# Thirty-two unused bytes in the constant pool of a one-core encoder layer

## The chip, the cores and the metric

The kernel runs on one core of one Trainium2 chip. The metric is the device time of the whole program in microseconds, here the median of three runs. A profile of one execution stands beside it: for each engine every instruction with its start, its duration, the source line, the tiles it writes and reads, and what ended the idle time before it. TensorE appears in it twice: PE is the streaming of a matmul's moving operand, PEld is the loading of the stationary operand (the weights) of the next matmul, which runs beside it. The other engines are DVE (VectorE), ACT (ScalarE), POOL (GpSimd) and SP, which issues most of the DMAs.

## The reference

One encoder layer is applied to two sequences of 1024 rows and 1024 columns, in fp32. Attention and a Fourier mixing run side by side, then a SwiGLU feed-forward layer follows. The feed-forward layer, which takes most of the time, is this:

```python
D_MODEL, SEQ = 1024, 1024
D_FF = int(math.ceil(8 * D_MODEL / 3 / 256) * 256)      # 2816

def layer(x, c, ...):
    ...
    mix = jnp.concatenate([y_mla, y_four], axis=-1) @ w_out
    x = x + ga1 * mix
    h2 = rmsnorm(x, g_ffn) * (1.0 + sc2) + sh2
    ffn = (jax.nn.silu(h2 @ w_gate) * (h2 @ w_up)) @ w_down
    return x + ga2 * ffn

y_prompt = rmsnorm(layer(x_prompt, c_prompt, ...), g_final)
y_sample = rmsnorm(layer(x_sample, c_sample, ...), g_final)
```

## The kernel before

**Precision.** Every fp32 operand of a large matmul is split into a high part (rounded to the type fp32r) and the rest: `split` (lines 60 to 63) writes `hi` with a ScalarE cast (L62) and `lo` with a VectorE subtraction (L63). A product is then three matmuls into the same PSUM bank, written by `mm3`:

```python
def mm3(out, lh, ll, rh, rl, first, last, cont=False):
    nc.tensor.matmul(out, lh, rh, start=first, stop=False, ...)      # L78
    nc.tensor.matmul(out, lh, rl, start=False, stop=False, ...)      # L79
    nc.tensor.matmul(out, ll, rh, start=False, stop=last, ...)       # L80
```

The second argument of `matmul` is the stationary operand, 128 columns of it; the third is the moving operand, as a rule 512 columns. So lines 78 to 80 carry most of TensorE's work, and the tile names in the profile tell the stages apart.

**Stages.** In order of time: the adaLN vectors, projections and the Fourier sums (0 to about 335 us), attention with the output projection (to about 797 us), then the feed-forward layer for sequence 0 and for sequence 1. Each feed-forward layer has two halves, and both use a Strassen-Winograd scheme, with seven products of half-size matrices in place of eight.

*Gate and up* (797 to 1237 us and 1449 to 1888 us). The seven combinations of the layer's input stand in SBUF for the whole half, each as two tiles of 4 x 512 columns, `H[k][0]` and `H[k][1]` (named H00 to H61, H in the profile). For each of 22 blocks of weights, `combos` loads the tile `rgu` (a slot named X0 or X1) and makes the sums on POOL into tiles `val`; `hl` splits each of the seven into `wh` and `wl`; and `prod` runs twelve matmuls for each of the seven:

```python
def prod(ps, k, wt, first):
    wh, wl = wt
    for c in range(4):
        cs = slice(c * P, c * P + P)
        mm3(ps, wh[:, cs], wl[:, cs], H[k][0][:, c, :], H[k][1][:, c, :], ...)
```

The weights are stationary, H moves. Between the products DVE adds bank and `val` (L137) and ACT copies a bank (L1311) before the same bank is added to again. The splits for block n+1 are written into the program beside the products of block n, so they run one block ahead; there are eight buffers each of `wh` and `wl`.

*Down* (1237 to 1449 us and 1888 us to the end). `prod2` loads two tiles of 512 columns for each step into a slot X0 or X1 (`draw` in the profile), splits both through `hl`, and multiplies `wh`/`wl` of the one by `wh`/`wl` of the other. At the end of sequence 1 the last of the seven products takes its operands, stationary and moving, from tiles that were split in advance into H slots (`held`).

**Where tiles lie.** Tiles come from pools on two sides of SBUF. A pool on the left grows from low addresses: first the constants (`const`), then small scalars (`tiny`), then one stage pool after another, in the feed-forward layer `p5` with the H and X slots. A pool with `side="right"` hangs from the top of SBUF: in the feed-forward layer `p5b` with `val`, `wh`, `wl`, `gf` and `ga`; in attention `p3` with `qa`, `qp`, `p` and `pt`, and `p4` with `wv` and the tiles `o`. The allocator rounds every tile to a multiple of 32 bytes. Addresses of the built program, modulo 64 bytes (and in brackets modulo 512):

| tiles | side | before |
|---|---|---|
| H and X slots (`rgu`, `draw`, `held`) | left | 0 (448) |
| `wh`, `wl`, `val`, `gf`, `ga` | right | 32 (480) |
| `lat00`, `lat01` (keys of sequence 0), `ckv`, `ql`, `wq_h`, `wq_l` | left | 0 (448) |
| `lat10`, `lat11` (keys of sequence 1), `qa`, `qp`, `pt`, `wv`, `o` | right | 32 (480) |
| `wz_h`, `wz_l` (input projection) | left | 0 |
| `hh`, `hl` of even pairs / of odd pairs | left | 0 / 32 |
| `ident` | constant, first tile | 0 |

The 512-column steps of a tile are 2048 bytes and the 128-column steps 512 bytes, so a slice of H, `wh` or `wl` keeps its tile's value.

**Order.** No planner sets the order: the instructions of an engine stand as the program emits them, and the tile framework adds the waits.

Of the kernel before, what the change touches and what calls it, by code (L numbers as in the profile page):

```python
# [12 lines left out]
F32 = mybir.dt.float32  # L13
# [8 lines left out]
P = 128  # L22
# [30 lines left out]
def hybrid_encoder_kernel(ctx: ExitStack, tc: tile.TileContext, a: dict):  # L53
# [28 lines left out]
    const = ctx.enter_context(tc.tile_pool(name="const", bufs=1))  # L82
# [7 lines left out]
    mhalf = const.tile([P, 2], F32, name="mhalf")  # L90
    nc.gpsimd.memset(mhalf, -0.5)
    cmask = const.tile([P, 7], F32, name="cmask")
    nc.sync.dma_start(cmask, a["cmask"])

    def rstd(ms, n, rest=None):
# [1535 lines left out]
```

## Time and profile before

| | |
|---|---|
| time, median of 3 runs | 2117.27 us (2114.76 to 2119.18) |
| span of the profiled execution, first to last instruction | 2109.8 us |
| its own time with what lies around the span | not listed for it; the median less the span is 7.5 us |
| gate and up, sequence 0 / sequence 1 | 797 to 1237 us / 1449 to 1888 us |
| down, sequence 0 / sequence 1 | 1237 to 1449 us / 1888 to 2110 us |
| DMA traffic | 371.30 MB, 176 GB/s over the span |

Rows by line read: line, engine, operation, output<-inputs, shape, xcount | busy us of the group, mean ns of one | idle time of the engine just before them, and what ended it. In rows of matmuls the moving and the stationary tile stand behind the arrow in that order, except that a name that is both stands once; the end of a matmul is modelled, so the mean is longer than the distance from one start to the next, by the same amount for the same shape. Rows by window read: stretch, its length, then for each engine busy us (xcount), the granted TensorE clock, the DMA engines' busy share and GB/s. A window counts each instruction that overlaps it.

### The profile page before, as it was taken

The page shows a single profiled execution, that of the slowest core. Times are in us where ns is not written, and L with a number is a line of the kernel's source. Part 1 is how long each engine was busy: PE and PEld are TensorE (multiplying, and loading weights), DVE is VectorE, ACT ScalarE, POOL GpSimd, SP SyncE. Part 2 cuts the span into 40 slices and gives each one's busy share as a digit, 9 for nine tenths or more (in the row PEclk, how much of TensorE's full clock was granted, in tenths as well). Part 3 has the DMA queues.
Part 4 walks back from the last instruction along what each step waited for, and adds up shares of the span by engine and source line. Part 5 has one row for each costly group of instructions (what it writes and reads, how often), then busy time and mean ns, then how long its engine had stood idle before and what let it go on. Part 6 is the DMA issues. An engine that isn't in the chain of part 4 may idle for free. (4 is left out here: it accounts for less than half of the span.)

```text
span 2109.8 us, 28784 instructions
## 1 busy us (share of the span) xinstructions
PE 2033.0 (96%) x10044; PEld 1667.0 (79%) x10044; DVE 1414.4 (67%) x2087; ACT 906.0 (43%) x1763; POOL 828.6 (39%) x1018
## 2 busy tenths in 40 slices
PE   5899998999999999999999999999999999999998
PEld 2788876888888887788888888887788888888886
DVE  2657756766676678777677677777766666566685
ACT  2656534555565555232333346453233333336441
POOL 1455202111311314888778610235544454420142
PEclk8999999999999999999999999999999999999999
DMA  9575765544544455554554578674332232247772
GB/s 368 194 248 190 248 233 197 113 88 91 159 119 118 150 186 211 180 193 169 194 185 166 174 250 270 222 236 164 131 119 90 91 125 95 81 154 280 233 227 99
DMA packets 184254, 371.30 MB, mean 176 GB/s; under 512 B 19052, under 2 KB 58604, under 8 KB 181036
## 3 DMA queue, kind: packets, MB, share of 16 engines
q1 hardware_dynamic: 166252, 314.00, 44.1%
q0 software_dynamic: 17856, 55.45, 8.9%
q8 instruction: 79, 1.29, 0.2%
q14 instruction: 67, 0.55, 0.1%
HBM read 257.38 MB, written 120.39 MB: 179 GB/s over the span
## 5 line engine op out<-in xcount | busy, mean ns | idle before, releaser
L78 PE MATMUL bank<-H,wh 128*128 128x512 f32 x1232 | 489.6, 398 | 7.7 <-ACT val L1311 4.0
L80 PE MATMUL bank<-H,wl 128*128 128x512 f32 x1232 | 488.9, 397 | 1.4 <-DVE wl L63 1.4
L79 PE MATMUL bank<-H,wh 128*128 128x512 f32 x1232 | 489.0, 397 | 0.0
L137 DVE TENSOR_TENSOR val<-bank,val 128x512 f32<-128x512 f32 x244 | 167.1, 690 | 185.7 <-PE bank L80 178.6
L78 PEld LDWEIGHTS bank<-H,wh 128*128 128x128 f32 x1232 | 232.5, 189 | 66.8 <-ACT val L1311 5.4
L80 PEld LDWEIGHTS bank<-H,wl 128*128 128x128 f32 x1232 | 232.5, 189 | 57.9 <-DVE wl L63 1.7
L79 PEld LDWEIGHTS bank<-H,wh 128*128 128x128 f32 x1232 | 232.7, 189 | 56.2
L63 DVE TENSOR_TENSOR wl<-draw,wh 128x512 fp32r<-128x512 f32 x286 | 203.1, 744 | 82.7 <-ACT wh L62 80.7
L62 ACT CAST wh<-draw 128x512 fp32r<-128x512 f32 x286 | 168.8, 619 | 159.0 <-PE bank L79 83.0
L137 POOL TENSOR_TENSOR val<-val 128x512 f32<-128x512 f32 x58 | 82.9, 1438 | 366.3 <-DVE val L1412 187.6
L79 PE MATMUL bank<-wl,wh 128*128 128x512 f32 x572 | 223.8, 391 | 1.6 <-DVE wl L63 1.6
L80 PE MATMUL bank<-wh,wl 128*128 128x512 f32 x572 | 222.7, 389 | 0.0
L78 PE MATMUL bank<-wh 128*128 128x512 f32 x572 | 222.6, 389 | 0.0
L62 ACT CAST wh<-rgu 128x512 fp32r<-128x512 f32 x172 | 106.7, 621 | 269.7 <-PE bank L79 209.5
L62 ACT CAST wh<-val 128x512 fp32r<-128x512 f32 x133 | 82.2, 622 | 280.5 <-PE bank L79 249.1
L63 DVE TENSOR_TENSOR wl<-val,wh 128x512 fp32r<-128x512 f32 x133 | 141.5, 1066 | 85.6 <-ACT wh L62 85.5
L63 DVE TENSOR_TENSOR wl<-rgu,wh 128x512 fp32r<-128x512 f32 x172 | 169.4, 985 | 4.9 <-ACT wh L62 4.8
L134 POOL TENSOR_TENSOR val<-rgu 128x512 f32<-128x512 f32 x84 | 122.8, 1462 | 125.0 <-DMA rgu<-in_wgu_dram 108.8
L79 PEld LDWEIGHTS bank<-wl,wh 128*128 128x128 f32 x572 | 107.4, 188 | 27.3 <-DVE wl L63 5.3
L78 PEld LDWEIGHTS bank<-wh 128*128 128x128 f32 x572 | 107.4, 188 | 22.4
L80 PEld LDWEIGHTS bank<-wh,wl 128*128 128x128 f32 x572 | 107.4, 188 | 22.0
L134 POOL TENSOR_TENSOR val<-val 128x512 f32<-128x512 f32 x89 | 119.4, 1357 | 1.3
(332 smaller groups left out, 4051.2 us busy)
## 6 DMA issues: line engine op xcount, KB each, us to landing
rgu<-in_wgu_dram SPq DMA_DIRECT2D x86, 512.0 KB
draw<-s_d SPq DMA_DIRECT2D x143, 256.0 KB
s_d<-val POOLq DMA_DIRECT2D x88, 256.0 KB, 4.1
draw<-t_d SPq DMA_DIRECT2D x88, 256.0 KB
s_d<-val SPq DMA_DIRECT2D x66, 256.0 KB
draw<-in_w_down_dram SPq DMA_DIRECT2D x55, 256.0 KB
wada<-in_w_ada_dram SPq DMA_DIRECT2D x13, 1024.0 KB
xt<-in_x_dram SPq DMA_DIRECT2D x16, 512.0 KB
```

The costliest lines, as they stand in the source:

```text
L62: here["a"] = nc.scalar.copy(hi, src).ins
L63: here["v"] = nc.vector.tensor_tensor(out=lo, in0=src, in1=rd(hi), op=ALU.subtract).ins
L78: nc.tensor.matmul(out, lh, rh, start=first, stop=False, skip_group_check=cont)
L79: nc.tensor.matmul(out, lh, rl, start=False, stop=False, skip_group_check=cont)
L80: nc.tensor.matmul(out, ll, rh, start=False, stop=last, skip_group_check=cont)
L134: return eng.tensor_tensor(out=out, in0=x, in1=y, op=ALU.subtract).ins
L137: eng.tensor_tensor(out=out, in0=x, in1=y, op=ALU.add)
```

## The change

One tile of 128 x 8 fp32 (32 bytes in each partition) is added to the pool `const`, behind its first tiles. Nothing writes or reads it.

```diff
     cmask = const.tile([P, 7], F32, name="cmask")
+    const.tile([P, 8], F32, name="phase")
     nc.sync.dma_start(cmask, a["cmask"])
```

Every tile that is allocated behind it on the left side lies 32 bytes higher: 1087 tile allocations, among them every H and X slot, `lat00`, `lat01`, `ckv`, `ql`, `wq_h`, `wq_l`, `wz_h`, `hh` and the small scalars. The tiles on the right side, `ident`, `identr`, `mhalf` and `cmask` stay where they were. Modulo 64, H and X are then at 32 (modulo 512 at 480), as `wh`, `wl` and `val` are, and two left-side tiles keep their distance from each other. All 18430 instructions of the built program, their order on each engine and their operands' tiles and shapes are the same as before; line numbers behind line 92 grow by one.

## The prediction

> **What bounds the kernel now.** I read the page first, for the share of each engine, then the stretches of the feed-forward layer by window, then TensorE's rows by form inside them, and last what TensorE waits for.
>
> ```profile
> span 2109.8 us, 28784 instructions
> PE 2033.0 (96%) x10044; PEld 1667.0 (79%) x10044; DVE 1414.4 (67%) x2087; ACT 906.0 (43%) x1763; POOL 828.6 (39%) x1018
> L78 PE MATMUL bank<-H,wh 128*128 128x512 f32 x1232 | 489.6, 398 | 7.7 <-ACT val L1311 4.0
> ```
>
> TensorE is busy 96% of the span, and gate and up alone are 3 x 1232 = 3696 matmuls of 512 columns (L78 shown; L79 and L80 have as many). The windows tell whether anything else holds them up:
>
> ```profile
> core 0: us, PE busy (x), PEclk, DMA share, GB/s
> 860.00:1230.00 370.00, 370.00 (x1587) 1.00 0.52 179
> 1510.00:1880.00 370.00, 370.00 (x1588) 1.00 0.29 100
> 1240.00:1390.00 150.00, 150.00 (x664) 1.00 0.79 262
> ```
>
> The first two are gate and up of the two sequences, the third is down. TensorE has no idle time in any of them and the clock is fully granted. So a matmul's own spacing sets the time there. It is not the same: a window catches one matmul more than fits, so it is (370.0 + 0.4)/1587 = 233.4 ns in gate and up and (150.0 + 0.4)/664 = 226.5 ns in down. The rows of these windows say it again:
>
> ```profile
> L78 PE MATMUL bank<-H,wh 128*128 128x512 f32 x529 | 209.2, 396 | 0.0
> L80 PE MATMUL bank<-H,wl 128*128 128x512 f32 x529 | 209.2, 395 | 0.0
> L79 PE MATMUL bank<-H,wh 128*128 128x512 f32 x529 | 209.2, 395 | 0.0
> ...
> L79 PE MATMUL bank<-wl,wh 128*128 128x512 f32 x222 | 86.4, 389 | 0.0
> L80 PE MATMUL bank<-wh,wl 128*128 128x512 f32 x221 | 86.0, 389 | 0.0
> L78 PE MATMUL bank<-wh 128*128 128x512 f32 x221 | 86.0, 389 | 0.0
> ```
>
> Same shape, type, clock and order of three; 6 to 7 ns apart. What differs is where the operands lie. In gate and up the moving H is at 0 modulo 64 and the stationary `wh` and `wl` at 32; in down both are at 32. Is it the address, or something else of the stage? Three places tell. The product from `held` runs at the end, with both operands in the very H slots:
>
> ```profile
> L79 PE MATMUL bank<-H 128*128 128x512 f32 x44 | 17.1, 389 | 0.0
> ```
>
> At 0 and 0 it takes 389 again, so H slots are not slow in themselves. The scores of attention are one piece of code that runs on both sequences; only the moving keys change, from `lat00`/`lat01` at 0 (sequence 0, first three rows, 400 to 545 us) to `lat10`/`lat11` at 32 (sequence 1, last three, 550 to 764 us), against `qa` and `qp` at 32:
>
> ```profile
> L906 PE MATMUL ps_s<-lat,qp 128*128 128x512 f32 x39 | 15.4, 395 | 0.0
> L907 PE MATMUL ps_s<-lat,qp 128*128 128x512 f32 x39 | 15.4, 395 | 0.0
> L904 PE MATMUL ps_s<-lat,qa 128*128 128x512 f32 x38 | 15.0, 396 | 0.0
> ...
> L907 PE MATMUL ps_s<-lat,qp 128*128 128x512 f32 x64 | 25.1, 392 | 0.0
> L904 PE MATMUL ps_s<-lat,qa 128*128 128x512 f32 x64 | 25.1, 392 | 0.0
> L906 PE MATMUL ps_s<-lat,qp 128*128 128x512 f32 x64 | 25.0, 391 | 0.0
> ```
>
> Apart 395 to 396, equal 391 to 392: the same sign. And the input projection alternates, at 448 columns: `wz` moves from 0, and the stationary `hh` is at 0 for even pairs (first three rows, 199.9 to 204.5 us) and at 32 for odd ones (218.3 to 222.9 us).
>
> ```profile
> L78 PE MATMUL bank<-wz_h,hh 128*128 128x448 f32 x8 | 2.9, 368 | 0.0
> L79 PE MATMUL bank<-wz_l,hh 128*128 128x448 f32 x8 | 2.9, 368 | 0.0
> L80 PE MATMUL bank<-wz_h,hl 128*128 128x448 f32 x7 | 2.6, 368 | 0.0
> ...
> L78 PE MATMUL bank<-wz_h,hh 128*128 128x448 f32 x8 | 2.9, 363 | 0.0
> L79 PE MATMUL bank<-wz_l,hh 128*128 128x448 f32 x8 | 2.9, 363 | 0.0
> ```
>
> Here equal addresses are the slower case, by 5 ns. So the address matters, but which relation is good depends on the length of the stream. For 512 columns every place that I found says equal is faster.
>
> **The change part by part.** No instruction is added, removed or moved; only addresses change.
>
> *Gate and up.* H goes to 32 modulo 64 and 480 modulo 512, which is what both operands of down have. I take down's spacing. The step per matmul is 6 (395 to 389) to 6.9 ns (233.4 to 226.5); I take 6.6. 3696 x 6.6 ns = 24.4 us if each one gains it. Where TensorE waited, an earlier arrival only lengthens the wait:
>
> ```profile
> PE bank L78 <- ACT val L1311: 4.0, 2, 2.6
> PE bank L78 <- DVE val L137: 3.4, 3, 2.1
> ...
> PE bank L80 <- DVE wl L63: 1.4, 1, 1.4
> ```
>
> Each row is its total, the number of times and the longest: six waits in the whole execution, all outside the windows above, so in the first blocks of a sequence. A block is 84 matmuls, so it gains 84 x 6.6 ns = 0.55 us. At worst six blocks lose their gain, 3.3 us; at best none. A wait takes only what stands ahead of it in its block, so I take half, 1.6 us. Gain 22.8 us.
>
> Can the others keep up with a block of 19.05 instead of 19.6 us?
>
> ```profile
> 850.00:1237.00 387.00, 386.14 (x1655) 310.90 (x1656) 274.39 (x277) 118.26 (x199) 288.40 (x264) 1.00 0.52 177
> ...
> 1500.00:1888.00 388.00, 385.88 (x1648) 310.27 (x1647) 239.78 (x280) 116.92 (x196) 170.50 (x145) 1.00 0.29 103
> ```
>
> In the fuller one, sequence 0 (columns PE, PEld, DVE, ACT, POOL), POOL is busy 288.4 of 387 us, 75%, and DVE 71%. At 2.8% shorter blocks they come to 77% and 73%. The splits run a block ahead, so their cover is about 19 us deep, and rows without idle time show that nothing is late now. I take no new wait; one new wait like those above in every fourth block, at 1 us, would cost 11 us, and that is a rival below.
>
> *Attention.* The scores of sequence 0, five lines of 64 matmuls, get the addresses of sequence 1: 320 x 3.5 ns is 1.1 us. Of that I take 0.8, as TensorE waits now and then in this stage. The value product moves `pt` at 32 against `ckv`, which goes from 0 to 32. It is 768 matmuls of 256 columns, of which no row shows the equal case for these tiles. The nearest with both on the left side, equal before and after, is the absorbed query:
>
> ```profile
> L80 PE MATMUL gb<-pt,ckv 128*128 128x256 f32 x123 | 35.0, 285 | 0.0
> ...
> L80 PE MATMUL gb<-ql,wq_l 128*128 128x256 f32 x30 | 8.5, 284 | 0.0
> ```
>
> 284 equal against 285 apart (both 550 to 760 us): no difference, and I take 0. The bounds are those of the longer streams: 5 ns slower as at 448 columns (3.8 us) to 6.6 ns faster (5.1 us).
>
> *Everything else.* `wz` and `hh`, `ql` and `wq` shift together. The splits of down get both inputs at 32 instead of 0 and 32, and DVE, ACT and POOL read tiles on either side already:
>
> ```profile
> L63 DVE TENSOR_TENSOR wl<-draw,wh 128x512 fp32r<-128x512 f32 x286 | 203.1, 744 | 82.7 <-ACT wh L62 80.7 <-DMA draw<-t_d 1.3
> L63 DVE TENSOR_TENSOR wl<-rgu,wh 128x512 fp32r<-128x512 f32 x172 | 169.4, 985 | 4.9 <-ACT wh L62 4.8
> ...
> L137 DVE TENSOR_TENSOR val<-val 128x512 f32<-128x512 f32 x12 | 8.0, 684 | 0.0
> L63 DVE TENSOR_TENSOR wl<-H,wh 128x512 fp32r<-128x512 f32 x3 | 2.1, 689 | 0.0
> ```
>
> The first two rows are the splits whose addresses change, at means that hold many stretched ones. The last two show a plain subtraction or addition of that shape: equal (32 and 32) 684 ns, apart (0 and 32) 689 ns. DVE doesn't tell them apart by more than 1%, and if the equal case were slower by as much, 286 + 172 splits at 5 ns are 2.3 us of an engine that is busy 71%, under TensorE. DMA writes to the slots start 32 bytes later; their share in down is 0.79, so they could take a quarter longer before they bind. Cost nothing.
>
> *The sum.* 22.8 + 0.8 = 23.6 us less: the profiled span goes from 2109.8 to 2086 us. The median lies 7.5 us over that span, so 2117.3 - 23.6 = 2093.7, and I say 2094.
>
> **The rule that speaks against it.** The Trainium skill's page "TensorE: Matmul & The Clock Gate" (Step-by-step: what each phase is for) says that TensorE reads SBUF through two independent ports, one for the streamed operand and one for the weights, so that loading the next weights takes nothing from the running matmul. By that rule an address cannot matter, and the time would stay at 2117. The rows above, 396 against 389 with one shape and clock, contradict it as far as one execution can.
>
> **The rivals.**
>
> *Nothing happens.* The 6.6 ns belong to the stage and not to the address: while gate and up run, POOL and DVE read the same memory more than in down. For it: I compare stages of different surroundings. Against it: POOL is far busier in sequence 0 than in sequence 1 of gate and up (288 against 170 us in the rows above), yet both windows have 233.4 ns; and the scores differ between sequences by the address alone. Time 2117; 4%.
>
> *Equal is the slow case for H too.* The input projection shows equal addresses 5 ns slower. If a long run over one set of H rows followed that pattern instead of down's, 3696 x 5 ns = 18.5 us are added in gate and up and 3.8 us in the value product: 2140. The mechanism is one, a read of weights that falls on the same part of memory as the streamed row; it decides as soon as the rows `bank<-H,wh` go above 396. Against it stands `held`, which is equal, from H, with 512 columns, at 389. 3%.
>
> *Another engine takes over.* The matmuls get faster, but blocks become uneven: POOL's sums, stores and DVE's splits block each other, and every fourth of 44 blocks waits 1 us. 23.6 - 11 = 12.6 us less: 2105. For it: POOL at 77%, and six such waits are there now. Against it: none after the first blocks of a sequence. 5%.
>
> *The tiles don't move as told.* The built program has them moved, so this is only open where a tile that matters stayed; H did not. It joins the first rival.
>
> **How the numbers follow.** Forecast 88%, rivals 4, 3 and 5%. Its own range: all matmuls gain 6.9 ns, no wait eats any (25.5), scores 1.1, and values gain half of their best (2.5): 29 us, 2088. At the other end 6 ns with six blocks lost (22.2 - 3.3 = 18.9), values lose 3.8: 15 us, 2102. The three runs before spread by 2 us either way, within these. Faster by over 0.2% (4.2 us; about what a measurement of this kernel can tell from no change): forecast and third rival, 93%. Within 0.2%: the first rival, 4%. Slower: 3%.
>
> **What would show it.** Right: rows `bank<-H,wh` and `bank<-H,wl` at 389 instead of 395 to 396; windows inside gate and up without idle time and about 45 matmuls more in 370 us; rows of down, `held` and `wz` as they are; scores of sequence 0 at 391 to 392; no new releaser behind L78. Wrong: H rows still at 395 with all else equal (the address is not the cause), or at 389 with new idle time behind ACT, DVE or POOL (the third rival), or `gb<-pt,ckv` longer by more than 5 ns.

## The result, and the profile after

| | before | after |
|---|---|---|
| time, median of 4 runs | 2116.28 us (2114.76 to 2119.18) | 2098.30 us (2095.19 to 2101.20) |
| ratio after / before, 95% interval | | 0.9918 (0.9906 to 0.9930) |
| span of the profiled execution | 2109.8 us | 2096.1 us (its own time 2097.92) |
| a block of gate and up between the waits | 19.60 us | 19.04 us |

The kernel is 18.0 us faster. The forecast was 2094 us, 23.6 us less, and its range was 2088 to 2102.

The rows of gate and up first, from the groups of the whole page, with the rows of the value product from the list of TensorE's groups (columns as before: busy us, mean ns of one, idle time before):

```profile
L78 PE MATMUL bank<-H,wh 128*128 128x512 f32 x1232 | 483.7, 393 | 10.2 <-ACT val L1312 5.4
L80 PE MATMUL bank<-H,wl 128*128 128x512 f32 x1232 | 482.7, 392 | 1.9 <-DVE wl L63 1.9
L79 PE MATMUL bank<-H,wh 128*128 128x512 f32 x1232 | 482.9, 392 | 0.0
L80 PE MATMUL bank<-wh,wl 128*128 128x512 f32 x572 | 222.8, 389 | 0.0
...
L78 PE MATMUL gb<-pt,ckv 128*128 128x256 f32 x256 | 74.0, 289 | 0.0
L80 PE MATMUL gb<-pt,ckv 128*128 128x256 f32 x256 | 73.5, 287 | 0.0
L79 PE MATMUL gb<-pt,ckv 128*128 128x256 f32 x256 | 73.4, 287 | 0.0
```

The rows of the value product before, over the same 768 matmuls:

```profile
L78 PE MATMUL gb<-pt,ckv 128*128 128x256 f32 x256 | 73.2, 286 | 0.0
L80 PE MATMUL gb<-pt,ckv 128*128 128x256 f32 x256 | 72.8, 284 | 0.0
L79 PE MATMUL gb<-pt,ckv 128*128 128x256 f32 x256 | 72.7, 284 | 0.0
```

The scores of sequence 0 after (400 to 545 us), for the three lines that the prediction showed:

```profile
L907 PE MATMUL ps_s<-lat,qp 128*128 128x512 f32 x40 | 15.6, 391 | 0.0
L908 PE MATMUL ps_s<-lat,qp 128*128 128x512 f32 x40 | 15.6, 391 | 0.0
L905 PE MATMUL ps_s<-lat,qa 128*128 128x512 f32 x39 | 15.3, 392 | 0.0
```

The means over all 1232 hold the matmuls behind waits. Inside the dense stretch of sequence 1 (1510 to 1860 us) they don't, and there H has the very mean of down, 389:

```profile
L78 PE MATMUL bank<-H,wh 128*128 128x512 f32 x516 | 200.9, 389 | 0.0
L79 PE MATMUL bank<-H,wh 128*128 128x512 f32 x515 | 200.5, 389 | 0.0
L80 PE MATMUL bank<-H,wl 128*128 128x512 f32 x515 | 200.5, 389 | 0.0
```

In windows that is (350.0 + 0.4)/1546 = 226.6 ns a matmul, with no idle time. Down, in the third row, has (140.0 + 0.4)/619 = 226.8 ns; the first row is gate and up of sequence 0, (110.0 + 0.4)/487 = 226.7 ns:

```profile
core 0: us, PE busy (x), PEclk, DMA share, GB/s
870.00:980.00 110.00, 110.00 (x487) 1.00 0.57 188
1510.00:1860.00 350.00, 350.00 (x1546) 1.00 0.30 106
1240.00:1380.00 140.00, 140.00 (x619) 1.00 0.78 260
```

What TensorE waits for between 795 and 1900 us, each row with its total, number and longest:

```profile
PE bank L78 <- ACT val L1312: 5.4, 3, 3.1
PE bank L78 <- DVE val L138: 4.4, 4, 2.9
PE bank L79 <- DVE wl L63: 2.5, 3, 1.0
PE bank L80 <- DVE wl L63: 1.9, 2, 1.4
```

Before, the first two rows held 4.0 and 3.4 us, the third 1.0 and the fourth 1.4. So the matmuls reached the spacing that was forecast, and in this pair of profiles some of what they won came back as waiting.

The starts of single matmuls, read from the two traces, give where the time went. A stretch of gate and up runs here from the start of its first matmul to the start of its last, and down from there to the first matmul of the next gate and up, or to the end:

| stretch | before, us | after, us | difference |
|---|---|---|---|
| start to gate and up of sequence 0 | 797.4 | 798.8 | +1.4 |
| gate and up, sequence 0 | 439.8 | 431.3 | -8.5 |
| down, sequence 0 | 211.6 | 213.5 | +1.9 |
| gate and up, sequence 1 | 439.6 | 431.0 | -8.6 |
| down, sequence 1, to the end | 221.4 | 221.5 | +0.1 |

The sum is the difference of the spans, 13.7 us. It is less than the 18.0 us of the medians because single executions of the kernel before differ by 10 us (19 runs on one chip went from 2110.48 to 2120.89), and the profiled one was a quick one. So a term of one or two microseconds must be read from rows, not from a time.

### The profile page after: what moved, and what is told of

It is laid out like the page before. It is cut to its first block, busy times and chain, and to the rows that moved or that the text cites. A ratio compares the mean times of both kernels' runs of the same rounds, so it can differ in the third digit from the quotient of the medians.

```text
span 2096.1 us, 28784 instructions
## 1 busy us (share of the span) xinstructions
PE 2013.3 (96%) x10044; PEld 1669.9 (80%) x10044; DVE 1398.5 (67%) x2087; ACT 905.6 (43%) x1763; POOL 827.8 (39%) x1018
## 5 line engine op out<-in xcount | busy, mean ns | idle before, releaser
L78 PE MATMUL bank<-H,wh 128*128 128x512 f32 x1232 | 483.7, 393 | 10.2 <-ACT val L1312 5.4
L80 PE MATMUL bank<-H,wl 128*128 128x512 f32 x1232 | 482.7, 392 | 1.9 <-DVE wl L63 1.9
L79 PE MATMUL bank<-H,wh 128*128 128x512 f32 x1232 | 482.9, 392 | 0.0
L78 PEld LDWEIGHTS bank<-H,wh 128*128 128x128 f32 x1232 | 233.0, 189 | 62.5 <-DVE val L138 6.8
L79 PEld LDWEIGHTS bank<-H,wh 128*128 128x128 f32 x1232 | 233.2, 189 | 48.6
L78 PE MATMUL bank<-wh 128*128 128x512 f32 x572 | 222.9, 390 | 0.2 <-ACT wh L62 0.2
L63 DVE TENSOR_TENSOR wl<-val,wh 128x512 fp32r<-128x512 f32 x133 | 128.4, 968 | 73.0 <-ACT wh L62 72.8
L63 DVE TENSOR_TENSOR wl<-rgu,wh 128x512 fp32r<-128x512 f32 x172 | 158.3, 921 | 5.8 <-ACT wh L62 5.6
L78 PEld LDWEIGHTS bank<-wh 128*128 128x128 f32 x572 | 107.4, 188 | 23.1 <-ACT wh L62 0.6
L80 PEld LDWEIGHTS bank<-wh,wl 128*128 128x128 f32 x572 | 107.4, 188 | 21.8
```

The costliest lines, as they stand in the source:

```text
L63: here["v"] = nc.vector.tensor_tensor(out=lo, in0=src, in1=rd(hi), op=ALU.subtract).ins
L78: nc.tensor.matmul(out, lh, rh, start=first, stop=False, skip_group_check=cont)
L79: nc.tensor.matmul(out, lh, rl, start=False, stop=False, skip_group_check=cont)
L80: nc.tensor.matmul(out, ll, rh, start=False, stop=last, skip_group_check=cont)
```

## Experiments

Theory: the spacing of 512-column matmuls follows from the distance between the moving row and the weights in SBUF, and nothing else of the stage matters. The rivals that the runs are to tell apart: other engines' traffic; that H itself must lie at a certain place; that another period than 64 bytes counts. A second question is where the last 5 us of the forecast went.

### Bare matmuls at many distances

```diff
+    def run(n, d, s, count=48):
+        ps = pp.tile([P, 512], F32, tag="b", name=...)
+        for i in range(count):
+            w = st[:, s // 4 + 128 * (i % 4) : s // 4 + 128 * (i % 4) + 128]
+            nc.tensor.matmul(ps[:, :n], w, mv[:, d // 4 : d // 4 + n], start=(i == 0), stop=(i == count - 1))
```

> Leaves out the whole layer: both outputs are plain copies of the inputs, and TensorE runs groups of 48 fp32r matmuls from one moving and one stationary tile, with no other engine at work; each group has another distance in bytes between the start of the moving row and the first weight, for 512, 480, 448, 384, 256 and 128 columns. Theory (the distance between the two reads, modulo 64 bytes): at 512 columns the spacing is 226.7 ns at distances 0, 64 and 128 and 233.3 at 32 and 96, whichever of the two tiles is moved; at 448 columns 206 at 0 and 200 at 32. What lies between at 8, 16, 24, 40, 48 and 56 is open. Rival (the other engines' traffic makes the difference): one spacing for all distances at a given number of columns. Rival (absolute address of the moving tile): the distance 0 with both at 32 differs from the distance 0 with both at 0.

The names in the rows give columns (n), the moving offset (m) and the offset of the weights (s) in bytes. From the list of groups:

```profile
L70 PE MATMUL n512m000s32b<-mv,st 128*128 128x512 f32 x48 | 11.4, 397 | 0.0
L70 PE MATMUL n512m032s00b<-mv,st 128*128 128x512 f32 x48 | 11.4, 395 | 0.0
L70 PE MATMUL n512m064s00b<-mv,st 128*128 128x512 f32 x48 | 11.2, 392 | 0.0
L70 PE MATMUL n512m032s32b<-mv,st 128*128 128x512 f32 x48 | 11.1, 390 | 0.0
...
L70 PE MATMUL n448m032s00b<-mv,st 128*128 128x448 f32 x48 | 10.1, 369 | 0.0
L70 PE MATMUL n448m000s00b<-mv,st 128*128 128x448 f32 x48 | 10.1, 368 | 0.0
L70 PE MATMUL n448m064s00b<-mv,st 128*128 128x448 f32 x48 | 9.8, 362 | 0.0
...
L70 PE MATMUL n256m000s00b<-mv,st 128*128 128x256 f32 x48 | 5.9, 283 | 0.0
L70 PE MATMUL n256m032s00b<-mv,st 128*128 128x256 f32 x48 | 5.8, 279 | 0.0
```

With no other engine at work, 0 against 32 is slow whichever side is moved, and 32 against 32 is as fast as 0 against 0. The traffic rival and the rival of H's own place fall. Spacing from start to start, mean ns:

| moving minus weights, bytes | 0 | 8 | 16 | 24 | 32 | 48 | 56 | 64 | 96 | 128 |
|---|---|---|---|---|---|---|---|---|---|---|
| 512 columns | 226.7 | 233.5 | 231.7 | 233.2 | 233.2 | 233.3 | 230.2 | 228.9 | 233.6 | 233.4 |
| 448 columns | 206.4 | | 202.2 | | 206.4 | 203.0 | | 200.1 | 205.2 | |
| 256 columns | 119.9 | | 118.9 | | 116.7 | 118.3 | | 117.8 | 120.0 | |

(226.7 is the spacing of the first group behind its slow first matmuls.) The kernel's own distance before, -32 bytes or 224 modulo 256, is the row `n512m000s32b`: its last twenty matmuls are 233.3 ns apart. Groups of other lengths ran too: at 480 columns 216.7 ns at 0 and 16, 219.9 at 32 and 213.4 at 48; at 384 columns 173.4 to 175.4 at the four distances tried. Two things were not expected. 64 and 128 are not as good as 0, so the period is not 64. And at 448 columns 32 is as slow as 0: what made the odd pairs of the projection faster is not a distance of 32. At 256 columns, distance 0 costs 3.2 ns more than 32.

### The other side moved

```diff
                 gf = S["gf"]
+                w5.tile([P, 8], F32, name="pad")
```

> The other side is moved: H, X and everything on the left stay as before, and wh, wl, val go from 32 to 0 modulo 64. Theory (distance): gate and up as in the changed kernel, blocks of 19.04 us, rows bank<-H at 389 away from the waits; the value product in attention stays as before (284 to 286 ns, not 287 to 289), so the time is 1 to 2 us under the changed kernel's: about 2097. Rival (H itself has to lie at 32): blocks of 19.60 us and 2116.

2096.08 us (2092.08 to 2098.26), ratio 0.9900 (0.9874 to 0.9925) against the kernel before with 2113.21 in the same job. Blocks take 19.04 us, with H where it was. The value product is at 287, 285 and 285 ns, near its old 286, 284 and 284. The 1 to 2 us under the changed kernel can't be told from a spread of 6 us.

### The left side moved by 64, 96, 160 and 288 bytes

```diff
-    const.tile([P, 8], F32, name="phase")
+    const.tile([P, 16], F32, name="phase")
```

(16, 24, 40 and 72 columns of 4 bytes.)

> The unused tile has 64 bytes instead of 32, so the left side moves, but keeps its address modulo 64. Theory (modulo 64): blocks of 19.60 us, rows bank<-H at 395 to 396, time 2116 as before. Rival (any move of H away from its old place, or of the small scalars, does it; or the period is 128): blocks near 19.04 us and 2098.

> The unused tile has 96 bytes: modulo 64 as in the changed kernel (H and wh both at 32), modulo 128 they are 64 apart (H at 32, wh at 96). Theory (modulo 64 alone): as the changed kernel, blocks of 19.04 us, 2098. Rival (period 128 or longer): blocks between 19.1 and 19.6 us, time between 2100 and 2116; the Fourier rows bank<-wm,B, which are 64 apart before, have a mean of 392 and hint at something between.

> The unused tile has 160 bytes. H, X and wh, wl are all at 32 modulo 64, as in the changed kernel, but H lies 128 bytes from wh modulo 256. Theory after the bare runs (the distance counts modulo 256, and 128 is a slow one at 233.3 ns): blocks of 19.60 us, time 2114 as before, although the addresses agree modulo 64. Rival (modulo 64 decides, as the change puts it): blocks of 19.04 us and 2098.

> The unused tile has 288 bytes: H lies 256 bytes from wh modulo 512, 0 modulo 256. Theory (period 256): blocks of 19.04 us, time 2098 as the changed kernel, value product at 287 to 289. Rival (period 512 or longer in the kernel): blocks between 19.2 and 19.6 us and 2105 to 2115.

| bytes | H minus `wh`, modulo 64 / modulo 256 | block, us | time, us | ratio to before in its job |
|---|---|---|---|---|
| 0 (before) | 32 / 224 | 19.60 | 2113 to 2116 | 1 |
| 32 (the change) | 0 / 0 | 19.04 | 2098.30 | 0.9918 (0.9906 to 0.9930) |
| 64 | 32 / 32 | 19.60 | 2114.53 | 0.9995 (0.9984 to 1.0007) |
| 96 | 0 / 64 | 19.60, then 19.23 | 2100.16 | 0.9936 (0.9916 to 0.9955) |
| 160 | 0 / 128 | 19.52 | 2114.18 | 1.0000 (0.9990 to 1.0009) |
| 288 | 0 / 0 | 19.04 | 2094.26 | 0.9905 (0.9891 to 0.9919) |

Windows of 300 us inside gate and up of sequence 1, one row for each kernel, in the order 64, 96, 160, 288:

```profile
1560.00:1860.00 300.00, 300.00 (x1287) 1.00 0.29 103
```

```profile
1560.00:1860.00 300.00, 300.00 (x1312) 1.00 0.30 106
```

```profile
1560.00:1860.00 300.00, 300.00 (x1292) 1.00 0.29 101
```

```profile
1560.00:1860.00 300.00, 300.00 (x1326) 1.00 0.30 106
```

All four windows are full at the whole clock; only the count differs: 233.4, 229.0, 232.5 and 226.5 ns a matmul. With 160 bytes H and `wh` agree modulo 64, as the change asks for, and nothing is gained. So agreement modulo 64 is not enough; modulo 256 it is. That 32 bytes gave agreement modulo 256 too (448 + 32 = 480, the value of `wh` modulo 512) is what made the change work.

### Bare matmuls, the period and what ran before

```diff
+    for n in range(3):
+        run(512, 0, 0, 24)
+        one(f"q064f{'abc'[n]}", 64, 96)
+        run(512, 32, 0, 24)
+        one(f"q064s{'abc'[n]}", 64, 96)
+    for d in (0, 4, 64, 128, 192, 256, 320, 384, 448, 508, 512, 576, 1024):
+        run(512, 32, 0, 24)
+        one(f"r{d:04d}z", d, 96)
```

> Leaves out the layer, as the first bare run. 512 columns throughout. Groups of 96 at distance 64 follow 24 matmuls at distance 0 (names q064fa to q064fc) or 24 at distance 32 (q064sa to q064sc); then single groups at other distances, each behind 24 at distance 32. Theory (the distance sets which spacings can hold, and at 64 which one does hangs on what ran before, as the two feed-forward halves with 64 between them ran at 19.60 and at 19.23 us a block): q064f groups near 228.9 ns and q064s groups near 233, distances 0, 512 and 1024 at 226.7, 4 and 508 nearer to 227 than to 233, and 128 to 448 at 233 or mixed. Rival (period 64 with a drift in the first run): 64, 128, ... 448 all at 226.7 to 229 whatever ran before.

From the list of groups, the number in a name being the distance:

```profile
L76 PE MATMUL r0004z<-mv,st 128*128 128x512 f32 x96 | 22.9, 399 | 0.0
...
L76 PE MATMUL r0128z<-mv,st 128*128 128x512 f32 x96 | 22.6, 395 | 0.0
...
L76 PE MATMUL q064fa<-mv,st 128*128 128x512 f32 x96 | 22.2, 391 | 0.0
...
L76 PE MATMUL r0320z<-mv,st 128*128 128x512 f32 x96 | 22.1, 391 | 0.0
...
L76 PE MATMUL q064sa<-mv,st 128*128 128x512 f32 x96 | 22.1, 391 | 0.0
...
L76 PE MATMUL r0508z<-mv,st 128*128 128x512 f32 x96 | 21.9, 388 | 0.0
...
L76 PE MATMUL r0256z<-mv,st 128*128 128x512 f32 x96 | 21.9, 389 | 0.0
```

The distances that were tried repeat after 256 bytes. From start to start: 0, 256, 512 and 1024 at 226.9 to 227.1 ns; 64, 320 and 576 at 228.9 to 229.1; 128 and 384 at 233.3; 192 and 448 at 233.2. Around 0 it is not symmetric: 4 bytes behind (508) cost nothing, 227.0, and 4 bytes ahead cost most of all, 236.7; half of the expectation on them fell. What ran before does not matter here: 64 bytes gave 229.1 behind a fast group and 228.9 behind a slow one. That part of the theory fell too.

### 96 bytes once more

> The kernel with 96 bytes once more, for a second profile: its halves ran at 19.60 and 19.23 us a block, while the bare run at that distance (64) held 228.9 ns, which is 19.23 us a block, whatever ran before. If the pattern is settled anew at each start of a half, its blocks take 19.60, 19.23 or another steady value, not the same pair of halves as before; if it belongs to the code, sequence 0 is at 19.60 and sequence 1 at 19.23 again.

2100.93 us, one run, on another chip; this time both halves of gate and up ran at 19.23 us a block, where the first profile had 19.60 in sequence 0. It is one program, so at distance 64 the same code can hold two spacings, 233.3 and 228.9 ns, each in nearly all of the 19 blocks of a half that follow the waits. The kernel's ten runs on the first chip spread from 2094.64 to 2110.72, so the second chip alone does not make the difference. What settles the spacing was not found: the bare run gave only the faster one. At distance 0 every profile with it, six in all, had 19.04 in both halves, away from the waits.

### Where the rest went: evacuations ahead of splits

TensorE waits at L78 because a bank has to be copied (ACT) or added (DVE) before it is added to again, and these stand in their queues behind a split for the next block. The edit writes them ahead of it:

```diff
-                def step(j, ps, k, first, src=src):
+                def step(j, ps, k, first, src=src, evac=None):
                     prod(ps, k, cur[j], first)
+                    if evac is not None:
+                        evac()
...
-                step(1, y, 5, True)
-                u2 = val()
-                add(u2, y, p1, nc.vector)
+                step(1, y, 5, True, evac=lambda: (u2.append(val()), add(u2[0], y, p1, nc.vector)))
```

and likewise for products 0, 3 and 4.

> Addresses as before; in each block of gate and up the copy of a bank (product 0) and the additions of a bank (products 1, 3 and 4) are written ahead of the split of the next block that used to stand in front of them on ACT and DVE. Theory (the rest of the forecast gain went into waits: TensorE waits for a copy or an addition that is queued behind a split whose POOL sum is late): the rows 'bank L78 <- ACT val' and 'bank L78 <- DVE val' lose most of their 7.4 us in the feed-forward layer, so even with the old addresses the time falls by 5 to 8 us, to about 2107. Rival (the copy or addition is itself slow, or the sums would be late for anyone): the waits stay and the time is 2113.

> The same order with the changed kernel's addresses. Theory (waits took it): blocks of 19.04 us without the two new waits of about 0.5 us and with shorter first blocks, so gate and up gain the forecast 23 to 24 us against the same order with old addresses; with 1 to 2 us lost in attention the time is 21 to 23 us under that kernel, near 2086. Rival (waits are not it): the difference stays at 15 to 18 us.

> The same order, and the right side moved instead of the left, so that the value product of attention keeps its distance. Theory: as the kernel with the order and the left side moved, and 1 to 2 us under it, near 2085; value product rows at 284 to 286 ns. Rival (attention lost nothing by the addresses): the same time as that kernel within the spread.

With old addresses: 2115.83 us, ratio 1.0004 (0.9993 to 1.0015). The order gained nothing. The waits between 795 and 1900 us show why:

```profile
PE bank L78 <- DVE val L137: 6.8, 4, 2.8
PE bank L78 <- ACT val L1312: 2.8, 2, 2.5
```

They held 3.4 and 4.0 before: the wait went from ACT to DVE and its sum grew. The third block of sequence 0 lost its wait (21.27 to 19.60 us) and the second grew (21.73 to 26.54). So this change of order moves the waits and does not shorten them. With the new addresses the same order ran at 2095.56 us, 20.3 us under it (ratio to the kernel before 0.9909, 0.9889 to 0.9929), and with the right side moved at 2095.35 us (0.9909, 0.9891 to 0.9928). 20.3 lies between the two expectations; the time near 2086 did not come, since the order itself gave nothing. The rows of the value product are at 289, 287, 287 with the left side moved and at 286, 284, 283 with the right side moved, as expected; in the time, 0.2 us, it can't be seen.

What the profiles do show is the five blocks that hold the waits (the first three of sequence 0, the first and third of sequence 1), summed:

| order | addresses | sum of the five, us |
|---|---|---|
| as before | 19.52 to 19.60 us a block (before; 64 bytes; 160 bytes) | 115.4; 114.4; 118.3 |
| as before | 19.04 us a block (after; right side; 288 bytes) | 119.3; 116.6; 115.7 |
| as before | 96 bytes (19.60, then 19.23; both 19.23) | 120.8; 117.0 |
| evacuations first | 19.60 | 117.7 |
| evacuations first | 19.04 (left; right; all distances, below) | 118.6; 116.8; 117.1 |

Five blocks that each gained 0.56 us would be 2.8 us shorter. The blocks that have the waits are not: the means of the first two rows are 116.0 and 117.2 us. Whether they grow is not shown, since the sums within one row differ by 4 us.

One of the waits tells more. In the third block of sequence 1 TensorE waited 1.98 to 2.13 us for an addition by DVE in the four profiles with 19.52 or 19.60 us a block, and 2.75 to 2.93 us in the six with 19.04: it arrives earlier and waits longer. In the traces of before and after DVE is busy without a break ahead of that addition, and with the same work: a multiplication of 3.6 us (L1335 before, L1336 after), two operations of the final norm of sequence 0 with 2.4 us together (L1438, L1439) and a split of 2.2 us. So in these two traces DVE's own work sets the end of this wait, and it does not get shorter with the matmuls. The other waits were not followed up like this.

### All distances chosen

```diff
+        w.tile([P, 24], F32, name="padh")
         wuqT = w.tile([P, HEADS, QL], F32, tag="hh0", name="wuqT")
...
+        w.tile([P, 40], F32, name="padz")
         wz_h = w.tile([P, NC, DZ], F32R, name="wz_h")
...
+            e.tile([P, 8], F32, name="padl")     # ahead of lat00
+            e.tile([P, 56], F32, name="padc")    # ahead of ckv0
```

> Evacuations first and the right side moved (as e7), and two more distances chosen: lat00 and lat01 at distance 0 from qa and qp (scores of sequence 0 near 391 to 392 instead of 395), and hh of even pairs at the distance that odd pairs have from wz (363 instead of 368 ns); ckv and wz stay where they were modulo 256. Theory: 320 x 3.5 ns and 192 x 6 ns, together 2.3 us, where TensorE does not wait: 1 to 2 us under e7, near 2094. Rival (these stages wait for other engines): no difference from e7.

(e7 is the kernel with evacuations first and the right side moved.)

2093.68 us (2092.31 to 2099.01), ratio 0.9909 (0.9895 to 0.9923), as for the kernel without these pads. The score rows fell (390 and 392, from 395), and of the last three even pairs the first projection went from between 206.4 and 206.7 ns to between 200.0 and 200.4; the second, at the same distance, came to 201.0 in one pair and 210.3 in two. So here too one distance goes with two spacings, in a stage where other engines are at work. No version was shown to beat the changed kernel: 0.9900 to 0.9909 against 0.9918, with intervals that overlap.

## Why the prediction was right, and where it was off

- *The address sets the spacing.* Right, and shown: 389 in place of 395 to 396, 226.6 ns in place of 233.4, from either side, and in a program with nothing else in it. The rule of the Trainium skill that was weighed there ("TensorE: Matmul & The Clock Gate", Step-by-step: what each phase is for: two independent read ports) is not borne out in what was drawn from it, that an address cannot matter: the spacing with weights loaded beside the stream depends on where they lie, 226.9 ns at distance 0 and 233.3 at 128. Where the two reads get in each other's way, no run here shows.
- *The size of it.* 6.6 ns a matmul was taken and 0.55 us a block; 0.56 us was measured in each of the 39 blocks without a wait in the profile before, 21.8 us.
- *Modulo 64.* The evidence was read too narrowly. The scores, `held` and down agree modulo 512, not only modulo 64, and so did H after the change; that was noted, and not used as a condition. With 160 bytes the same argument would have forecast a gain where there is none. That 32 bytes met the condition that counts, and not only the one that was stated, was in part luck.
- *The input projection as a counterexample.* Its even pairs are at distance 0, its odd ones at 160 modulo 256. That equal addresses are the slow case at 448 columns is right (206.4 bare); that the fast one is "32 apart" is not (206.4 as well).
- *The waits.* The term that was mis-sized. 1.6 us was taken as lost, at most 3.3. The five blocks with waits did not lose part of their gain but all of it, 2.8 us (5 x 0.56), and in this pair of profiles they grew by 3.8 us besides; over all the profiles such growth is not shown. Two more blocks of sequence 0 ran 0.47 us longer each, at a new wait for an addition by DVE (0.17 us of idle time each). A longer wait can be dearer than itself, since the clock can fall behind it. The windows of ten microseconds around two of these waits, before and then after, have these clocks (column PEclk):

```profile
849.00:859.00 10.00, 8.59 (x37) 6.61 (x37) 7.41 (x6) 3.37 (x6) 9.29 (x10) 1.00 0.25 83
1500.00:1510.00 10.00, 7.88 (x28) 5.96 (x27) 9.58 (x9) 1.74 (x3) 6.67 (x5) 0.83 0.45 166
```

```profile
849.00:859.00 10.00, 8.12 (x29) 6.20 (x28) 3.96 (x4) 2.74 (x5) 9.51 (x10) 0.83 0.31 97
1495.00:1505.00 10.00, 7.08 (x20) 5.29 (x19) 9.41 (x8) 1.73 (x3) 7.47 (x6) 0.68 0.51 186
```

  In the profile after, the wait near 850 us has grown from 1.41 to 1.88 us and the clock is halved for a third of the window, and near 1500 us, where the wait grew from 2.12 to 2.92 us, for two thirds instead of one. The same page of the Trainium skill (Part 1: The HAM clock gate) says that the gate goes to half rate after an idle window of about 3.4 us that runs freely. The traces agree in the step and in the length, with halved stretches of 3.4 or 6.8 us, but not in the idle time ahead of them: the clock fell at waits of 1.88, 2.12 and 2.92 us, all shorter than that window. A wait of such a length does not always bring it about: with the evacuations first and the right side moved, the clock stayed whole behind one of 2.53 us.
- *Attention.* Scores as forecast, 391 to 392 in sequence 0 where they don't wait. The cost of the value product was taken as 0, from a row of the query product, 284 against 285; it lost 2.9 ns a matmul (287 to 289 from 284 to 286), 768 x 2.9 ns = 2.2 us. The bare run has the same sign and size, 119.9 against 116.7 ns. The two rows compared there were of products that wait on different things; the price of a distance can't be read across products of 6 and of 24 matmuls.
- *The sum in hindsight.* In the two profiles gate and up gained 21.8 us in the 39 blocks, lost 3.8 in the five with waits and 0.9 in the two with a new one: 17.1 us, the 8.5 and 8.6 of the table. The rest of the table is losses, 1.4 us ahead of it and 1.9 in down of sequence 0, for which the forecast had nothing. These two can't be laid to the addresses: over the twelve profiles of the kernel and its versions gate and up starts between 796.9 and 802.1 us and that half of down takes 211.6 to 213.5, with slow and with fast matmuls. With no growth in the five blocks the parts are 21.8 - 0.9 + 1.1 (scores) - 2.2 (values) = 19.8 us, against 18.0 measured. So the forecast's 23.6 was too high by about 2 us for the waits and 2 for attention; what is left is within the 2 to 4 us by which profiles differ.
- *The time around the span.* 7.5 us was worked out from a median and one execution. With its own time beside it, an execution has 1.8 us around its span (2097.92 less 2096.1), so the profiled execution of the kernel before was some 5 us under its median. It did not change the forecast, which was made on the difference.

Left open: why the period is 256 bytes and why 4 bytes ahead is worst, which no trace here shows; what settles the spacing at distance 64; and what ends the waits other than that of the third block of sequence 1. That DVE's work ends that one is read from the traces, and no run takes this work away.

## What to carry to other kernels

Where a dense row of matmuls of one shape has different means in two stages at the same clock, compare the addresses of the moving rows and of the weights modulo 256 before looking for another cause, and move one pool by a small unused tile to test it. Choose the distance for the shape that has most of the matmuls: 0 was best for 512 columns and worst of those tried for 448 and nearly so for 256. And count a gain only over the stretches without a wait; a stretch that ends at another engine's time need not get shorter.

## What the runs showed of the hardware that was not expected

- The distance counts modulo 256 bytes, not 64, for 512 fp32r columns: 226.9 ns at 0, 229 at 64, 233.3 at 128 and 192.
- It is not symmetric: 227.0 ns at -4 bytes (508), 236.7 ns at +4.
- At some distances one program has two steady spacings: 233.3 and 228.9 ns at 64, through 19 blocks of 84 matmuls; 200 and 206 ns in the projection at 448 columns.
